# Two-layer hybrid transformer on one core: adaLN steps issued between blocks of the second product, and GpSimd's subtractions moved to VectorE

## The chip, the cores and the metric

The kernel runs on one core of a Trainium2 chip. The metric is device time in microseconds (us), the median of the runs. A profiled execution is one run with the hardware profiler on. Engines are named as in the profile: PE (TensorE), DVE (VectorE), ACT (ScalarE), POOL (GpSimd) and SP (SyncE, whose queue issues most DMAs).

## The reference, cut to what matters

```
def swiglu(h, wi, wo):
    g, u = jnp.split(h @ wi, 2, axis=-1)
    return (jax.nn.silu(g) * u) @ wo
def ffn_step(t, sh, sc, g, wi, wo):
    return t + 0.5 * g * swiglu(modulate(rms(t), sh, sc), wi, wo)
...
mod_l = (jax.nn.silu(c) @ ada_w[i] + ada_b[i])[:, None, :]     # 9 vectors of 1024: shift, scale, gate x 3
mod_c = jax.nn.silu(c_ctx) @ ada_w[i] + ada_b[i]
x = ffn_step(x, sh1, sc1, g1, pre_wi, pre_wo)                  # half-step
x = x + g2 * mixer(modulate(rms(x), sh2, sc2), ...)            # attention and its output projection
x = ffn_step(x, sh3, sc3, g3, post_wi, post_wo)                # half-step
```

This is done for two layers. The stream has 512 latent and 256 context tokens of width 1024 (the last half-step: the latent tokens alone), and the inner width of a half-step is 2816. All is float32.

## The kernel before, in words

The stream `x` stays in SBUF as 8 chunks of 128 features by 768 tokens. Each float32 factor of a product is split in a high and a low part (`split`: ACT casts the high part, DVE subtracts to get the low one, line 74 for weights), and each product is three matmuls. So every weight slab of 128x1024 costs two casts on ACT and two subtractions on DVE (tiles `whi` and `wlo`).

There are four half-steps (`ffn`): layer 0 pre and post, layer 1 pre and post. Each runs over 22 chunks `f` of the inner width. Chunk `f` of the first product is `up(f)` (tile `ps_up`). Chunks 0 to 2 use the normed activations plainly (line 522); from chunk 3 on a product with 7 in place of 8 multiplications is used (line 456), for which each chunk needs 4 sums of weight quarters (tile `s`, lines 442 to 445) and the whole half-step needs 3 sums of activation quarters (`Seven.sums`: tiles `both`, `t`, `T1` to `T3` with high and low parts, made after chunk 1, and `Seven.replace` after chunk 2). After chunks 4, 8, 12, 16 and 20 the second product `down(g)` of four earlier chunks follows (tile `ps_dn`, line 569), in four weight slabs of four blocks each; DVE adds each block to `x` times the gate (line 390). After chunk 21 comes the last `down`.

`Norm` makes a half-step's normed activations chunk by chunk while the product before it ends: DVE multiplies (`xs`), ACT adds the shift and casts (`h_h`), and the low part `h_l` is made by POOL for feature chunks 1, 3 and 5 (line 373, behind two ACT instructions) and by DVE for the others (line 376).

The adaLN vectors need a matrix-vector product with `ada_w` for two conditions. Most of it is cut into steps (`Halves`): a step loads a 128x512 piece (`wh`, by SP, three buffers) and DVE multiplies it with the conditions and sums along the row (line 253, tiles `junkh` and `wh`; two multiplies a step, one where only latent tokens need the vector). Steps are issued by `beside`, after a chunk of the first product, from chunk 1 on:

```
                halves(Q0, seven.pool)      # Q0, Q1, Q2 = 6, 4, 5 steps after each chunk 1 to 19
```

The framework orders each engine's instructions by a planned timeline; instructions marked with `keep` (the DMAs of the steps among them) keep their place in the order in which the code issues them. On each engine, and in SP's queue, instructions run in the order that results.

Of the kernel before, what the change touches and what calls it, by code (L numbers as in the profile page):

```python
# [17 lines left out]
P = 128  # L18
# [24 lines left out]
def hybrid_backbone_kernel(ctx: ExitStack, tc: tile.TileContext, I, out):  # L43
# [175 lines left out]
    class Halves:  # L219
# [6 lines left out]
        def add(self, l, ms):  # L226
            def bias(m):
                md = const.tile([P, 2, KC], F32, name=f"mod{l}_{m}")
                mods[l][m] = md[:, 0], md[:, 1], md
                b = adab[:, l, m * KC:(m + 1) * KC].unsqueeze(1).broadcast_to([P, 2, KC])  # L230
                if m in (1, 4, 7):
                    nc.gpsimd.tensor_scalar_add(md, b, 1.0)
                else:
                    nc.gpsimd.tensor_copy(md, b)

            def silu(q):
                cs = []
                for nm in ("c", "c_ctx"):
                    t = small.tile([P, 512], F32, name="ch", tag="ar", bufs=3)
# [5 lines left out]
            def job(pool, q, m, d):  # L245
# [3 lines left out]
                w = pool.tile([P, 512], F32, name="wh", tag="wh", bufs=3)  # L249
                keep(nc.sync.dma_start(w, I["ada_w"][l, m * KC + d, :, q * 512:(q + 1) * 512]))  # L250
                for ty in types:
                    o = w if ty == types[-1] else small.tile([P, 512], BF16, name="junkh", tag="tmp", bufs=4)
                    nc.vector.scalar_tensor_tensor(o, w, 1.0, self.c[ty], ALU.mult, ALU.mult,  # L253
                                                   accum_out=self.part[:, ty, d:d + 1])
                if d == KC - 1:
                    md, n = mods[l][m][2], len(types)
                    nc.gpsimd.tensor_add(md[:, :n], md[:, :n], self.part[:, :n])  # L257
                    if q == 1 and m in (2, 8):
                        nc.gpsimd.tensor_scalar_mul(md[:, :n], md[:, :n], 0.5)

            for q in range(2):
                for m in ms:
                    for d in range(KC):
                        def f(pool, q=q, m=m, d=d):
                            if q == 0 and d == 0:
                                bias(m)
                            if m == ms[0] and d == 0:
                                silu(q)
                            job(pool, q, m, d)
                        self.steps.append(f)  # L270

        def __call__(self, n, pool):
            for _ in range(min(n, len(self.steps))):
                self.steps.pop(0)(pool)

# [33 lines left out]
    class Norm:  # L309
# [53 lines left out]
        def chunk(self, p, d):  # L363
            s0, n, ty, _ = self.parts[p]
            tk = slice(s0, s0 + n)
            sh, sc = (mods[self.l][self.msh + i][ty][:, d:d + 1] for i in range(2))
            hi, lo = self.reg.hi[:, d, tk], self.reg.lo[:, d, tk]
            xs = small.tile([P, 256], F32, name="xs", tag="tmp", bufs=4)
            nc.vector.scalar_tensor_tensor(xs, x[:, d, tk], sc, self.r[p], ALU.mult, ALU.mult)  # L369
            if d % 2 and d < 7:  # L370
                nc.scalar.activation(xs, xs, AF.Identity, bias=sh)
                nc.scalar.copy(hi, xs)
                nc.gpsimd.tensor_sub(lo, xs, hi.bitcast(F32))
            else:
                nc.scalar.activation(hi, xs, AF.Identity, bias=sh)
                nc.vector.scalar_tensor_tensor(lo, xs, sh, hi.bitcast(F32), ALU.add, ALU.subtract)


    turns = [0]

    def into_x(group, pieces, gate, product, follow=None):

        slabs = [load_slab(src) for src, _ in group]
        for s0, n, ty, parts in pieces:
            for i, (_, ds) in enumerate(group):
                for dd, d in enumerate(ds):
# [5 lines left out]
                    if follow is not None:  # L392
                        for p in parts:
                            follow(p, d)


    class Seven:
# [13 lines left out]
        def sums(self, pool):  # L411
# [87 lines left out]

    def ffn(l, msh, w1, w2, nt, norm, pool, after_up, follow, side, beside=None, feed=None):  # L500

# [57 lines left out]
        def down(g):  # L559
# [4 lines left out]
            def product(ps, w, i, d, s0, n):  # L564
                for fi, f in enumerate(fs):
                    wh, wl = w.cols(fi * dper * P + i * P, P)
                    ah, al = acts[f]
                    for k, (wv, a) in enumerate(((wh, ah), (wh, al), (wl, ah))):
                        nc.tensor.matmul(ps, wv, a[:, s0:s0 + n], start=fi == 0 and k == 0,  # L569
                                         stop=fi == nf - 1 and k == 2)  # L570

            jobs = [(w2[4 * g + s], list(range(s * dper, (s + 1) * dper))) for s in range(nf)]
            last = fs[-1] == NF - 1
            for group in ([jobs] if last else [[j] for j in jobs]):
                into_x(group, parts_of(nt) if last else halves, mods[l][msh + 2], product, follow if last else None)

# [145 lines left out]

    def oproj(l, oh, ol, w, nt, norm):
        def product(ps, wt, i, d, s0, n):
# [6 lines left out]
        for ds in ([0], [1], [2], [3], [4], [5], [6, 7]):  # L731
            into_x([(w[d], [d]) for d in ds], parts_of(nt) if len(ds) > 1 else halves_of(nt), mods[l][5], product,
                   norm.follow)

# [351 lines left out]
    halves = Halves()  # L1086
    Q0, Q1, Q2 = 6, 4, 5
    h0 = Norm(0, 0, T, "right", "h0_")
# [9 lines left out]
    with tc.tile_pool(name="f0", bufs=1) as pool:  # L1098
# [47 lines left out]
        halves.add(0, (2,))  # L1146
        halves.add(0, range(3, NMOD))

        def beside(f, seven):
            if f == 0:  # L1150
                start_cm.__exit__(None, None, None)
            elif f < NF - 2:
                if f == 17:
                    load_gains(0, "a")
                    load_rest(small)
                halves(Q0, seven.pool)
        ffn(0, 0, I["pre_wi"][0], I["pre_wo"][0], T, h0, pool, up_done, h1.follow, "right", beside, feed)
# [124 lines left out]
```

## Time and profile before

| | |
|---|---|
| median of 3 runs | 2940.08 us (2938.19 to 2943.32) |
| profiled execution | 2939.59 us, span 2937.8 us |
| PE busy | 2733.8 us, 93% of the span |
| DVE busy | 2229.2 us, 76% |
| ACT, POOL busy | 1229.8 us (42%), 498.3 us (17%) |
| mean granted PE clock | 0.979 |

PE is busy nearly always, and the shares are averages over stages: what limits a stage is read from the windows and waits of that stage. The granted clock is a share of the full one: 1.0 stands for 2.4 GHz and 0.5 for 1.2 GHz.

### The profile page before, as it was taken

Reading aid. Unit: us, or ns where it says so; the run is one execution under the profiler, and the core shown is the slowest. Engines: PE = TensorE matmul, PEld = TensorE weight load, DVE = VectorE, ACT = ScalarE, POOL = GpSimd, SP = SyncE. Lnnn points to the kernel's source line nnn. Section 1 sums busy time; section 2 is a strip of 40 time slices with the busy share of each in tenths; the row PEclk is TensorE's granted clock in tenths of the full one; section 3 lists DMA queues with packets and bytes.
Section 4 is the critical chain, followed back from the end, with each engine's and each line's share of the span. In section 5 each row is a group of like instructions: output and inputs, shape, how many; then the busy total and the mean of one; then the engine's idle time right before and its main releaser. Section 6 shows DMA issues by size and latency. Waiting matters only on the chain.

```text
span 2937.8 us, 47517 instructions
## 1 busy us (share of the span) xinstructions
PE 2733.8 (93%) x17948; PEld 2589.0 (88%) x17948; DVE 2229.2 (76%) x4613; ACT 1229.8 (42%) x3053; POOL 498.3 (17%) x586
## 2 busy tenths in 40 slices
PE   4799899999999989799999989999999999999999
PEld 3698898889999978789999978999998999999999
DVE  7988987877677756877886598787766766488887
ACT  4423222336556644323333343332334566454443
POOL 5300000025433422200000051000002521220000
PEclk9899999999999999899999999999999999999999
DMA  6333433322011022233332223343322101223333
GB/s 209 114 127 129 133 125 101 119 79 73 30 30 34 26 85 73 86 108 115 109 114 65 72 76 115 126 133 112 100 73 89 45 29 30 73 78 101 98 93 101
DMA packets 98709, 266.49 MB, mean 91 GB/s; under 512 B 12592, under 2 KB 16688, under 8 KB 98352
## 3 DMA queue, kind: packets, MB, share of 16 engines
q1 hardware_dynamic: 91968, 251.78, 26.8%
q10 hardware_dynamic: 6512, 11.68, 1.2%
q8 instruction: 141, 2.31, 0.3%
q14 instruction: 88, 0.72, 0.1%
HBM read 256.07 MB, written 7.34 MB: 90 GB/s over the span
## 4 chain that ended last, share of the span: by engine, by line
PE 66%; DVE 22%; issue 4%; DMA 4%; ACT 2%; POOL 1%; SPq 0%; ACTq 0%; DVEq 0%; POOLq 0%
PE ps_up L456 24%; PE ps_dn L569 22%; PE ps_qkv L651 7%; DVE wlo L74 4%; PE ps_dn L728 4%; DVE wh L253 3%; DVE junkh L253 2%; PE ps_av L989 2%; PE ps_up L522 2%; DMA wh<-in_ada_w 2%; DVE xs L369 1%; DMA raw<-in_pre_wi 1%; PE ps_av L825 1%; PE ps_s L781 1%; PE ps_pt L978 1%
## 5 line engine op out<-in xcount | busy, mean ns | idle before, releaser
L73 ACT CAST whi<-raw 128x512 fp32r<-128x512 f32 x556 | 341.4, 620 | 765.5 <-PE ps_dn L569 318.0
L569 PE MATMUL ps_dn<-ah,whi 128*128 128x256 f32 (+1 forms) x1456 | 463.3, 321 | 2.6 <-DVE x L390 1.8
L74 DVE TENSOR_TENSOR wlo<-raw,whi 128x512 fp32r<-128x512 f32 x556 | 402.9, 729 | 79.9 <-ACT whi L73 68.4
L569 PE MATMUL ps_dn<-al,whi 128*128 128x256 f32 (+1 forms) x1456 | 462.0, 319 | 0.1
L569 PE MATMUL ps_dn<-ah,wlo 128*128 128x256 f32 (+1 forms) x1456 | 454.1, 319 | 0.2 <-DVE wlo L74 0.2
L456 PE MATMUL ps_up<-h_h,whi 128*128 128x384 f32 (+1 forms) x1216 | 400.9, 330 | 38.7 <-ACT whi L73 25.9
L456 PE MATMUL ps_up<-h_h,wlo 128*128 128x384 f32 (+1 forms) x1216 | 394.3, 328 | 12.9 <-DVE wlo L74 12.8
L456 PE MATMUL ps_up<-h_l,whi 128*128 128x384 f32 (+1 forms) x1216 | 397.8, 327 | 0.0
L390 DVE SCALAR_TENSOR_TENSOR x<-ps_dn,mod,x 128x256 f32<-128x256 f32 (+1 forms) x442 | 241.9, 556 | 142.5 <-PE ps_dn L569 101.9
L73 ACT CAST whi<-s 128x512 fp32r<-128x512 f32 x304 | 188.1, 620 | 266.9 <-PE ps_up L456 221.9
L569 PEld LDWEIGHTS ps_dn<-ah,whi 128*128 128x128 f32 x1456 | 276.1, 191 | 25.3 <-ACT whi L73 2.5
L569 PEld LDWEIGHTS ps_dn<-al,whi 128*128 128x128 f32 x1456 | 277.5, 191 | 19.6 <-DVE al L74 0.3
L569 PEld LDWEIGHTS ps_dn<-ah,wlo 128*128 128x128 f32 x1456 | 275.9, 191 | 19.4 <-DVE wlo L74 0.4
L456 PEld LDWEIGHTS ps_up<-h_h,whi 128*128 128x128 f32 x1216 | 233.1, 192 | 47.1 <-ACT whi L73 27.2
L456 PEld LDWEIGHTS ps_up<-h_h,wlo 128*128 128x128 f32 x1216 | 232.2, 192 | 15.1 <-DVE wlo L74 15.0
L74 DVE TENSOR_TENSOR wlo<-s,whi 128x512 fp32r<-128x512 f32 x304 | 208.2, 687 | 41.7 <-ACT whi L73 38.0
L456 PEld LDWEIGHTS ps_up<-h_l,whi 128*128 128x128 f32 x1216 | 233.0, 192 | 0.5
L651 PE MATMUL ps_qkv<-whi,h_h 128*128 128x256 f32 x704 | 205.4, 292 | 4.3 <-DVE a L607 3.6
L651 PE MATMUL ps_qkv<-wlo,h_h 128*128 128x256 f32 x704 | 199.7, 286 | 1.9 <-DVE wlo L74 1.9
L651 PE MATMUL ps_qkv<-whi,h_l 128*128 128x256 f32 x704 | 200.3, 285 | 0.0
L257 POOL TENSOR_TENSOR mod<-mod,part 128x16 f32<-128x16 f32 (+1 forms) x32 | 14.7, 460 | 1065.4 <-DVE wh L253 1031.5
L253 DVE SCALAR_TENSOR_TENSOR wh<-wh,ch 128x512 f32<-128x512 f32 x256 | 185.5, 733 | 1.7 <-DMA wh<-in_ada_w 1.5
(226 smaller groups left out, 6684.9 us busy)
## 6 DMA issues: line engine op xcount, KB each, us to landing
wh<-in_ada_w SPq DMA_DIRECT2D x256, 256.0 KB, 3.7
raw<-in_pre_wi SPq DMA_DIRECT2D x88, 512.0 KB, 3.5
raw<-in_post_wi SPq DMA_DIRECT2D x88, 512.0 KB, 3.5
raw<-in_pre_wo SPq DMA_DIRECT2D x44, 512.0 KB, 3.5
raw<-in_post_wo SPq DMA_DIRECT2D x44, 512.0 KB, 3.5
raw<-in_a_w_qk SPq DMA_DIRECT2D x16, 512.0 KB, 3.5
araw<-in_ada_w SPq DMA_DIRECT2D x12, 512.0 KB, 4.5
raw<-in_a_w_v SPq DMA_DIRECT2D x8, 512.0 KB, 3.5
```

The costliest lines, as they stand in the source:

```text
L73: nc.scalar.copy(hi, src)
L74: nc.vector.tensor_sub(lo, src, hi.bitcast(F32))
L253: nc.vector.scalar_tensor_tensor(o, w, 1.0, self.c[ty], ALU.mult, ALU.mult, accum_out=self.part[:, ty, d:d + 1])
L369: nc.vector.scalar_tensor_tensor(xs, x[:, d, tk], sc, self.r[p], ALU.mult, ALU.mult)
L390: nc.vector.scalar_tensor_tensor(x[:, d, s0:s0 + n], ps, gate[ty][:, d:d + 1], x[:, d, s0:s0 + n], ALU.mult, ALU.add)
L456: nc.tensor.matmul(ps, ww, z[:, k, :n], start=first and k == 0 and i == 0, stop=k == 3 and i == 2, skip_group_check=True)
L522: nc.tensor.matmul(ps, w, h[:, k, s0:s0 + n], start=k == 0 and i == 0, stop=k == KC - 1 and i == 2)
L569: nc.tensor.matmul(ps, wv, a[:, s0:s0 + n], start=fi == 0 and k == 0, stop=fi == nf - 1 and k == 2)
L651: nc.tensor.matmul(ps, h[:, k, bt], w, start=n == 0, stop=n == 23)
L728: nc.tensor.matmul(ps, wv, o[:, k, s0:s0 + n], start=k == 0 and j == 0, stop=k == KC - 1 and j == 2)
L781: nc.tensor.matmul(sv[:, u], Q[:, c, qt], K[:, c, kb0 * P + u * half:kb0 * P + (u + 1) * half], start=i == 0, stop=i == 1)
L989: nc.tensor.matmul(po[:, j], a[:, k, j], V[:, kb, g], start=k == 0, stop=k == len(kbs) - 1)
```

## The change

Steps are no longer issued in equal numbers after each chunk. `beside(first, early)` issues none after chunks 1 to `first` (3), save in the first half-step (5, 5 and 6 steps after chunks 1, 2 and 3), and one after each later chunk; `between(n)` spreads `n` steps (13, 10 and 13 in the three half-steps) over the 16 blocks of each of the first five second products. The ninth vector's 16 steps of layer 0 move from the first half-step into the output projection of the first attention, two after each of its first 8 blocks, in buffers of tag `st`. The operations of a step are as before. Apart from that, all low parts of `Norm`, the other half of the `both` sums and the low parts of `T1` to `T3` go from POOL to DVE, and `Norm`'s chunks 1, 3 and 5 lose one ACT instruction each.

```diff
-        def __call__(self, n, pool):
+        def __call__(self, n, room):
             for _ in range(min(n, len(self.steps))):
-                self.steps.pop(0)(pool)
+                self.steps.pop(0)(room)
+
+        def beside(self, first, early=()):
+            def f(i, seven):
+                if i:
+                    self(early[i - 1] if i <= len(early) else int(i > first), (seven.pool, "wh", 3))
+            return f
+
+        def between(self, n):
+            def f(i, seven):
+                self((i + 1) * n // 16 - i * n // 16, (seven.pool, "wh", 3))
+            return f
...
-            if d % 2 and d < 7:
-                nc.scalar.activation(xs, xs, AF.Identity, bias=sh)
-                nc.scalar.copy(hi, xs)
-                nc.gpsimd.tensor_sub(lo, xs, hi.bitcast(F32))
-            else:
-                nc.scalar.activation(hi, xs, AF.Identity, bias=sh)
-                nc.vector.scalar_tensor_tensor(lo, xs, sh, hi.bitcast(F32), ALU.add, ALU.subtract)
+            nc.scalar.activation(hi, xs, AF.Identity, bias=sh)
+            nc.vector.scalar_tensor_tensor(lo, xs, sh, hi.bitcast(F32), ALU.add, ALU.subtract)
...
                     if follow is not None:
                         for p in parts:
                             follow(p, d)
+                    if tick is not None:
+                        tick()
...
-                    (nc.vector if i else nc.gpsimd).tensor_add(r[:, :2 * n], self.hi[:, kk, :2 * n].bitcast(F32),
+                    nc.vector.tensor_add(r[:, :2 * n], self.hi[:, kk, :2 * n].bitcast(F32),
                                          self.lo[:, kk, :2 * n].bitcast(F32))
...
                     nc.scalar.copy(th[:, k, :n], t)
-                    nc.gpsimd.tensor_sub(tl[:, k, :n], t, th[:, k, :n].bitcast(F32))
+                    nc.vector.tensor_sub(tl[:, k, :n], t, th[:, k, :n].bitcast(F32))
...
+            blocks = iter(range(16))
+            def tick():
+                if between is not None and fs[-1] < NF - 1:
+                    between(next(blocks), seven)
...
-        halves.add(0, range(3, NMOD))
+        halves.add(0, range(3, NMOD - 1))
+        others = halves.beside(3, (5, 5, 6))
...
-        oproj(0, o.hi, o.lo, I["a_w_o"], T, h2)
+        halves.add(0, (NMOD - 1,))
+        oproj(0, o.hi, o.lo, I["a_w_o"], T, h2, lambda: halves(2, (pool, "st", 5)))
...
-            lambda f, seven: halves(Q1, seven.pool) if 0 < f < NF - 2 else None)
+            halves.beside(3), halves.between(10))
...
-            lambda f, seven: halves(Q2, seven.pool) if 0 < f < NF - 2 else None)
+            halves.beside(3), halves.between(13))
```

What this does to the order is seen at three places. On DVE in the second half-step, at chunks 1 to 3, the quarter sums (`t`, `both`) stood among adaLN multiplies before:

```order
L427 TENSOR_TENSOR t<-both,t 128x384
L424 TENSOR_TENSOR t<-both 128x384
L253 SCALAR_TENSOR_TENSOR wh,part<-wh,ch 128x512 x2
L253 SCALAR_TENSOR_TENSOR junkh,part<-wh,ch 128x512
L425 TENSOR_TENSOR t<-both,t 128x384
L555 TENSOR_TENSOR sg<-sg,ps_up 128x512
L426 TENSOR_TENSOR t<-both 128x384
L74 TENSOR_TENSOR wlo<-raw,whi 128x512
L253 SCALAR_TENSOR_TENSOR wh,part<-wh,ch 128x512
```

Now the same sums stand there without multiplies, and with the low parts `T1l` to `T3l` that POOL made before:

```order
L438 TENSOR_TENSOR t<-both,t 128x384
L439 TENSOR_TENSOR t<-both 128x384
L437 TENSOR_TENSOR t<-both 128x384
L443 TENSOR_TENSOR T1l<-t,T1h 128x384
L74 TENSOR_TENSOR al<-sg,ah 128x256
L440 TENSOR_TENSOR t_12694<-both,t 128x384
L443 TENSOR_TENSOR T2l<-t,T2h 128x384
L74 TENSOR_TENSOR wlo<-raw,whi 128x512
L438 TENSOR_TENSOR t<-both,t 128x384
L443 TENSOR_TENSOR T3l<-t,T3h 128x384
```

Second, on DVE in the same half-step at the end of chunk 12, just ahead of a second product (its first `x` is the first block's sum), there was no multiply before:

```order
L483 TENSOR_TENSOR u<-u,ps_up 128x384
L74 TENSOR_TENSOR wlo<-raw,whi 128x512
L485 TENSOR_TENSOR u<-u,ps_up 128x384
L74 TENSOR_TENSOR wlo<-raw,whi 128x512
L487 TENSOR_TENSOR u<-u,ps_up 128x384
L74 TENSOR_TENSOR wlo<-raw,whi 128x512
L465 TENSOR_TENSOR u<-u 128x384
L74 TENSOR_TENSOR al<-u,ah 128x384
L491 TENSOR_TENSOR u<-u,ps_up 128x384
L74 TENSOR_TENSOR wlo<-raw,whi 128x512
L390 SCALAR_TENSOR_TENSOR x<-ps_dn,mod_8_2888,x 128x512
```

Now most multiplies of the steps that the code issues inside that second product stand ahead of it, where 16 of them lie between chunk 11's and chunk 12's last addition of a product (the line that was 487 and is now 504):

```order
L255 SCALAR_TENSOR_TENSOR wh,part<-wh,ch 128x512 x2
L255 SCALAR_TENSOR_TENSOR junkh,part<-wh,ch 128x512
L255 SCALAR_TENSOR_TENSOR wh,part<-wh,ch 128x512
L255 SCALAR_TENSOR_TENSOR junkh,part<-wh,ch 128x512
L500 TENSOR_TENSOR u<-u,ps_up 128x384
L255 SCALAR_TENSOR_TENSOR junkh,part<-wh,ch 128x512
L74 TENSOR_TENSOR wlo<-raw,whi 128x512
L255 SCALAR_TENSOR_TENSOR wh,part<-wh,ch 128x512
L478 TENSOR_TENSOR u<-u 128x384
L255 SCALAR_TENSOR_TENSOR wh,part<-wh,ch 128x512
L504 TENSOR_TENSOR u<-u,ps_up 128x384
L74 TENSOR_TENSOR wlo<-raw,whi 128x512
```

Third, in SP's queue around a second product of the first half-step, the four weight slabs (`raw` from `pre_wo`) were mostly loaded one behind the other before:

```order
L94 DMA raw<-in_pre_wo 128x1024
L250 DMA wh<-in_ada_w 128x512 x3
L94 DMA raw<-in_pre_wo 128x1024 x3
L94 DMA raw<-in_pre_wi 128x1024 x2
L250 DMA wh<-in_ada_w 128x512 x5
```

Now three pieces of `ada_w` stand between each two of them:

```order
L94 DMA raw<-in_pre_wo 128x1024
L252 DMA wh<-in_ada_w 128x512 x3
L94 DMA raw<-in_pre_wo 128x1024
L252 DMA wh<-in_ada_w 128x512 x3
L94 DMA raw<-in_pre_wo 128x1024
L252 DMA wh<-in_ada_w 128x512 x3
L94 DMA raw<-in_pre_wo 128x1024
```

## Rows read from the trace of the kernel before

**Rows 1.** The page: busy time of each engine; DVE's busy tenths in 40 slices.

```profile
PE 2733.8 (93%) x17948; PEld 2589.0 (88%) x17948; DVE 2229.2 (76%) x4613; ACT 1229.8 (42%) x3053; POOL 498.3 (17%) x586
...
DVE  7988987877677756877886598787766766488887
```

**Rows 2.** Stretches: length; busy PE, PEld, DVE, ACT, POOL; PE clock; DMA share; GB/s.

```profile
171.70:575.80 404.10, 379.72 (x2114) 356.62 (x2112) 334.59 (x756) 126.22 (x228) 5.36 (x10) 0.98 0.38 120
1253.70:1630.40 376.70, 367.37 (x2076) 346.05 (x2075) 292.67 (x601) 123.00 (x222) 3.15 (x7) 1.00 0.32 101
1816.10:2187.80 371.70, 366.11 (x2080) 346.45 (x2080) 276.85 (x546) 122.84 (x222) 3.65 (x9) 1.00 0.34 111
2095.20:2187.80 92.60, 92.48 (x530) 88.26 (x529) 59.83 (x104) 31.06 (x56) 0.00 (x0) 1.00 0.23 69
1061.90:1136.00 74.10, 72.06 (x460) 65.25 (x458) 26.92 (x46) 20.44 (x45) 17.97 (x22) 0.98 0.21 61
84.40:145.10 60.70, 43.49 (x238) 37.63 (x237) 57.99 (x111) 20.49 (x43) 23.27 (x16) 0.87 0.36 109
1137.70:1218.30 80.60, 63.04 (x356) 55.43 (x356) 76.79 (x139) 35.39 (x78) 33.71 (x27) 0.87 0.26 79
1717.00:1784.60 67.60, 53.67 (x295) 46.50 (x294) 65.73 (x116) 26.81 (x59) 29.94 (x23) 0.90 0.29 94
2560.00:2613.50 53.50, 44.22 (x300) 42.32 (x300) 46.98 (x81) 28.28 (x65) 24.38 (x24) 0.84 0.21 68
575.80:615.30 39.50, 38.21 (x218) 33.93 (x218) 28.89 (x64) 8.47 (x16) 0.48 (x2) 1.00 0.27 81
```

**Rows 3.** PE's waits from 58 to 2262 us: total us, times, longest.

```profile
PE ps_up L456 <- ACT whi L73: 30.2, 11, 12.5
PE ps_up L456 <- DVE wlo L74: 18.4, 7, 4.9
PE ps_up L456 <- ACT u L464: 12.9, 14, 2.2
PE ps_up L456 <- DVE u L483: 10.8, 12, 3.3
```

**Rows 4.** Chain that ended last, first half-step: start us, us, what.

```profile
257.14 14.76 PE ps_up L456 x82
```

**Rows 5.** Timeline, second half-step, chunks 1 to 3: start us, us, instruction, [idle before].

```profile
1200.10 1.19 POOL L430 TENSOR_TENSOR T2l<-t,T2h 128x384 fp32r<-128x384 f32 x1 [1.03 <-ACT T2h L429]
...
1200.34 1.50 DVE L253 SCALAR_TENSOR_TENSOR wh<-wh,ch 128x512 f32<-128x512 f32 x1
...
1206.97 0.69 PE L456 MATMUL ps_up<-h_h,wlo 128*128 128x384 f32 x1 [4.77 <-DVE wlo L74]
...
1207.45 0.68 DVE L253 SCALAR_TENSOR_TENSOR junkh<-wh,ch 128x512 bf16<-128x512 f32 x1
...
1208.06 0.55 DVE L425 TENSOR_TENSOR t<-both,t 128x384 f32<-128x384 f32 x1
...
1208.53 0.55 DVE L426 TENSOR_TENSOR t<-both 128x384 f32<-128x384 f32 x1
...
1218.36 0.69 PE L456 MATMUL ps_up<-h_h,whi 128*128 128x384 f32 x1 [7.82 <-ACT whi L73]
```

**Rows 6.** Timeline of PE, third half-step, chunk 3.

```profile
1783.33 0.69 PE L456 MATMUL ps_up<-h_h,whi 128*128 128x384 f32 x1 [5.62 <-ACT whi L73]
```

**Rows 7.** Timeline of DVE, second half-step, three instructions merged in each.

```profile
1138.06 1.27 DVE L369 SCALAR_TENSOR_TENSOR xs<-x,mod,ar 128x256 f32<-128x256 f32 x3
...
1167.96 2.68 DVE L420 TENSOR_TENSOR both<-h_h,h_l 128x768 f32<-128x768 f32 x3
```

**Rows 8.** Groups of POOL by shape: xcount, busy us, mean ns, idle before.

```profile
L373 POOL TENSOR_TENSOR h_l<-xs,h_h 128x256 fp32r<-128x256 f32 x42 | 35.0, 833 | 33.4 <-ACT h_h L372 31.5 <-PE ps_up L522 1.3
...
L420 POOL TENSOR_TENSOR both<-h_h,h_l 128x768 f32<-128x768 f32 x12 | 26.4, 2209 | 5.6 <-DVE t L426 3.8 <-DVE mod L217 1.8
...
L430 POOL TENSOR_TENSOR T1l<-t,T1h 128x384 fp32r<-128x384 f32 x12 | 16.6, 1387 | 54.7 <-ACT T1h L429 54.7
```

**Rows 9.** The page's DMA issues: KB each, median us to landing.

```profile
wh<-in_ada_w SPq DMA_DIRECT2D x256, 256.0 KB, 3.7
```

More of the change, by code (lines that the diff above doesn't have):

```diff
@@ L234, in bias, with silu @@
                     nc.gpsimd.tensor_copy(md, b)
-            def silu(q):
+            def silu(room, q):
                 cs = []
                 for nm in ("c", "c_ctx"):
-                    t = small.tile([P, 512], F32, name="ch", tag="ar", bufs=3)
+                    pool, tag, bufs = (small, "ar", 3) if room[1] == "wh" else room
+                    t = pool.tile([P, 512], F32, name="ch", tag=tag, bufs=bufs)
                     keep(nc.sync.dma_start(t, I[nm][q * 512:(q + 1) * 512].partition_broadcast(P)))
@@ L243, in silu, with job @@
                 self.c = cs
-            def job(pool, q, m, d):
+            def job(room, q, m, d):
                 types = (0, 1) if l == 0 or m < 5 else (0,)
@@ L248, in job @@
                     self.part = small.tile([P, 2, KC], F32, name="part", tag="part", bufs=2)
-                w = pool.tile([P, 512], F32, name="wh", tag="wh", bufs=3)
+                pool, tag, bufs = room
+                w = pool.tile([P, 512], F32, name="wh", tag=tag, bufs=bufs)
                 keep(nc.sync.dma_start(w, I["ada_w"][l, m * KC + d, :, q * 512:(q + 1) * 512]))
@@ L263, in add, with f @@
                     for d in range(KC):
-                        def f(pool, q=q, m=m, d=d):
+                        def f(room, q=q, m=m, d=d):
                             if q == 0 and d == 0:
@@ L267, in f @@
                             if m == ms[0] and d == 0:
-                                silu(q)
-                            job(pool, q, m, d)
+                                silu(room, q)
+                            job(room, q, m, d)
                         self.steps.append(f)
-        def __call__(self, n, pool):
+        def __call__(self, n, room):
             for _ in range(min(n, len(self.steps))):
-                self.steps.pop(0)(pool)
+                self.steps.pop(0)(room)
[8 more added lines that the diff above has]
+            return f
     def rstd_steps(sq, s_n, n, use, room=None):
@@ L369, in chunk, with into_x @@
             nc.vector.scalar_tensor_tensor(xs, x[:, d, tk], sc, self.r[p], ALU.mult, ALU.mult)
-            if d % 2 and d < 7:
-                nc.scalar.activation(xs, xs, AF.Identity, bias=sh)
-                nc.scalar.copy(hi, xs)
-                nc.gpsimd.tensor_sub(lo, xs, hi.bitcast(F32))
-            else:
-                nc.scalar.activation(hi, xs, AF.Identity, bias=sh)
-                nc.vector.scalar_tensor_tensor(lo, xs, sh, hi.bitcast(F32), ALU.add, ALU.subtract)
+            nc.scalar.activation(hi, xs, AF.Identity, bias=sh)
+            nc.vector.scalar_tensor_tensor(lo, xs, sh, hi.bitcast(F32), ALU.add, ALU.subtract)
     turns = [0]
-    def into_x(group, pieces, gate, product, follow=None):
+    def into_x(group, pieces, gate, product, follow=None, tick=None):
         slabs = [load_slab(src) for src, _ in group]
@@ L498, in hybrid_backbone_kernel, with ffn @@
     EARLY = 1
-    def ffn(l, msh, w1, w2, nt, norm, pool, after_up, follow, side, beside=None, feed=None):
+    def ffn(l, msh, w1, w2, nt, norm, pool, after_up, follow, side, beside=None, between=None, feed=None):
         seven = None
@@ L574, in down @@
             for group in ([jobs] if last else [[j] for j in jobs]):
-                into_x(group, parts_of(nt) if last else halves, mods[l][msh + 2], product, follow if last else None)
+                into_x(group, parts_of(nt) if last else halves, mods[l][msh + 2], product, follow if last else None,
+                       tick)
         for f in range(NF):
@@ L720, in finish, with oproj @@
                 self.tick()
-    def oproj(l, oh, ol, w, nt, norm):
+    def oproj(l, oh, ol, w, nt, norm, tick=None):
         def product(ps, wt, i, d, s0, n):
@@ L732, in oproj @@
             into_x([(w[d], [d]) for d in ds], parts_of(nt) if len(ds) > 1 else halves_of(nt), mods[l][5], product,
-                   norm.follow)
+                   norm.follow, tick)
     def diff_attention(norm, O, pool, save, finish_proj, ready):
@@ L1086, in hybrid_backbone_kernel @@
     halves = Halves()
-    Q0, Q1, Q2 = 6, 4, 5
     h0 = Norm(0, 0, T, "right", "h0_")
@@ L1151, in beside @@
                 start_cm.__exit__(None, None, None)
-            elif f < NF - 2:
+            else:
                 if f == 17:
@@ L1155, in beside @@
                     load_rest(small)
-                halves(Q0, seven.pool)
-        ffn(0, 0, I["pre_wi"][0], I["pre_wo"][0], T, h0, pool, up_done, h1.follow, "right", beside, feed)
+                if f < NF - 1:
+                    others(f, seven)
+        ffn(0, 0, I["pre_wi"][0], I["pre_wo"][0], T, h0, pool, up_done, h1.follow, "right", beside, halves.between(13), feed)
     o = attention_phase(0, h1, T)
```

## The prediction

> **What bounds the kernel now.** I read the page first: PE is busy 93% of the span, VectorE 76%, but VectorE's slices run from 6 to 9 tenths [rows 1], so the question is which stages wait for it. PE's waits say it: in the stretch with the first three half-steps, the longest sums end with weights that ACT or VectorE prepares (30.2 and 18.4 us) and with ACT's and VectorE's work on the products (12.9 and 10.8) [rows 3]. ACT is no bound (42%); its casts wait for VectorE's quarter sums. The windows then show two kinds of stage [rows 2].
>
> Steady cycles: four chunks of the first product and one second product. The cycle from 2095.2, which has no adaLN step, takes 92.6 us with PE busy 92.48. Four of them would take 370.4. The first half-step's four, with 6 steps beside nearly every chunk, take 404.1: 33.7 us too many, with VectorE busy 335 of them. In the second and third half-step (4 and 5 steps a chunk) PE idles 376.7 - 367.4 = 9.3 and 371.7 - 366.1 = 5.6.
>
> Starts, where the quarter sums of the activations are made beside chunks 1 to 3: VectorE is busy 58.0 of 60.7, 76.8 of 80.6 and 65.7 of 67.6 us there, and PE waits 4.77 and then 7.82 us for the first two weights of chunk 3 in the second half-step [rows 5], 5.62 in the third [rows 6]. The granted clock is 0.87 to 0.90 in these windows, against 1.00 in undisturbed cycles, so part of the matmuls after such a wait run at half rate.
>
> **What the change costs and saves on VectorE.** Issued back to back, a multiply of a step takes 0.61 us (1207.45 to 1208.06), a subtraction of 384 columns 0.47 [rows 5], one of 768 0.89, a norm operation of 256 0.42 [rows 7]. But the multiply that starts 0.24 us after GpSimd's T2l took 1.50 us, where 0.68 is usual, and ended 0.55 after it: it was held up until GpSimd was done [rows 5]. In the second half-step's start I count in the order 24 multiplies, 39 norm operations, 20 of 384, 4 of 768, 19 of 512 and 9 smaller; at 0.60 for 512 and 0.32 for the small ones they need 14.6 + 16.4 + 9.4 + 3.6 + 11.4 + 2.9 = 58.3 us, and VectorE was busy 76.8. The other 18.5 is delay beside GpSimd, whose 25 instructions there go to VectorE for 9 x 0.42 + 4 x 0.89 + 12 x 0.47 = 13.0 us, in place of 0.83, 2.21 and 1.39 us each on GpSimd [rows 8].
>
> The Trainium skill, SBUF — State Buffer, section "SBUF: two separate sides", says that VectorE with two SBUF inputs and GpSimd take their shared port pair as an exclusive lock for a whole instruction. The row agrees in kind. By the rule the loss could reach 9 x 0.83 + 4 x 2.21 + 12 x 1.39 = 33 us in this start, against the 18.5 that the windows give; the sum would gain no more by it, since PE becomes the bound there before.
>
> Term 1, steady cycles: 33.7 + 9.3 + 5.6 = 48.6 us can be won. In the first half-step the last 14 of the 16 moved steps leave these cycles, and in all three the rest stands mostly in the chunk ahead of a second product and beside the blocks. I leave 1 us for each of the 12 cycles: 48.6 - 12 = 36.6. If VectorE stays late as often as now, nothing is won: bounds 0 and 48.6.
>
> Is there room for the hoisted group? Between the last additions of chunks 11 and 12 VectorE now has 16 multiplies, 9.8 us, beside 8 us of its usual work, so some 18 us, where a chunk takes PE 14.8 [rows 4]. It falls 3 us behind there, but the two weights that the second product begins with stand before the bulk of the group, and its first slab feeds four blocks, a quarter of a second product of 92.6 - 4 x 14.76 = 33.6 us: 8.4 us of cover. If that cover is gone, 3 us come back each time.
>
> Term 2, start of the second half-step: out go 24 multiplies (14.6) and the 18.5 of delay, in come 13.0. VectorE's 76.8 becomes 56.7, with the 3.8 it idled 60.5, so it reaches the second weights of chunk 3 at 1137.7 + 60.5 = 1198, where PE arrives at about the same time as now (it began chunk 3 at 1201.7). PE runs the first of seven products (2.1 us), then meets five subtractions still ahead of it (3 us): second product at 1204, not 1218.4, 14.4 earlier. The group of multiplies ahead of the first second product comes right behind this without cover built up; I give back 1.0. Gain 13.4, bounds 7 and 20 (all idle time from 1136 to 1253).
>
> Term 3, third half-step: 23 multiplies (14.0) leave and the delay, 65.7 less the 48.6 that the order's instructions need, counted in the same way, 17.1; 10.8 comes. VectorE arrives 20 us earlier, at 1764, before PE can (1775.6 less what PE waits in chunks 0 to 2, some 9). Second product at 1767 + 5 = 1772, against 1783.3, less 1.3: gain 10, bounds 5 and 17.
>
> Term 4, first half-step: it keeps 16 of its 18 steps beside chunks 1 to 3, so 31 multiplies stand there for 32; 9.2 of low parts come, 58.0 - 44.9 (counted likewise) = 13.1 of delay goes: 4.5 earlier. Behind it, 18 multiplies stand beside chunk 4. Bounds -3 and 10.
>
> Term 5, last half-step: no steps, but the same sums and norm. PE idles 9.3 of 53.5 us at clock 0.84 [rows 2]. I take a third, 3, bounds 0 and 7. Term 6, the norms that lead into the two attentions lose one ACT instruction and a GpSimd subtraction of 0.83 us [rows 8] per odd chunk: 2, bounds 0 and 4.
>
> At nothing: the 16 steps in the output projection are 32 x 0.61 = 19.5 us of VectorE, which idles 47 of that window's 74.1 [rows 2]; uncovered they would cost 19.5. DMA bytes are unchanged.
>
> Sum: 36.6 + 13.4 + 10 + 4.5 + 3 + 2 = 69.5. The profiled execution's own time is 2939.59 (1.8 over its span, 0.5 under the median of the runs shown), so 2939.6 - 69.5 = **2870**. All upper bounds give 48.6 + 20 + 17 + 10 + 7 + 4 = 107, so 2833; all lower ones 0 + 7 + 5 - 3 + 0 + 0 = 9, so 2931.
>
> **The rivals.** (a) The groups of multiplies ahead of the 15 second products are not covered: VectorE is 3 to 6 us late at each, say 3, so 45 come back: 2915. For it: the multiplies are issued between blocks, but the order puts most of them before, so the change does less than it says; and single chunks lose time now at 18 to 19 us of VectorE work. Against it: the slack of 8.4 us. (b) VectorE's stretched instructions have another cause than GpSimd, and it is simply full. Then the delays of 18.5, 17.1 and 13.1 stay: 69.5 - 48.7 = 21, so 2919. The Trainium skill, Perfetto Trace Analysis, section "Optimizing Scalar/DVE Operations", speaks for this side: when VectorE is saturated, work may be offloaded to GpSimd; it adds that their shared port can undo that, which the 1.50 us row shows. (c) Slower: in SP's queue a weight slab of the second product now stands behind three adaLN pieces, and each of these waits until VectorE has emptied its buffer; a piece lands 3.7 us after its issue [rows 9]. With 15 second products of three later slabs each, a slab late by 69.5 / 45 = 1.5 us eats all; at 3 us late the time is 2939 + 66 = 3005. Against it: the second product from 575.8 already runs with three pieces between slabs, and PE idles 1.3 us of 39.5 in it [rows 2]. (d) More: the cycles become clean and the starts lose their slow clock: 2845 or less.
>
> **How the numbers follow.** Forecast, gain 50 to 90: 0.60. (d) 0.13. (a), partly or whole, 0.14; (b) 0.06; (c) 0.05; no change that could be measured 0.02. A measurement of this kernel tells about 0.2%, 6 us, from no change. So faster 0.93, same 0.02, slower 0.05. The range leaves out the ends of (d), (c) and part of (a) and (b): 2838 to 2910.
>
> **What would show it.** Right: adaLN multiplies absent from chunks 1 to 3 of the second and third half-step, no quarter sum on GpSimd, VectorE's multiplies back at 0.68 us there, PE's wait for chunk 3's second weights under 2 us, cycles of 93 to 95 us, clock near 1.0 after chunk 0. Wrong: waits of the second product's first matmuls for `wlo` or of VectorE for pieces of `ada_w`, or PE idle around chunks 4, 8, 12 and 16. What makes it wrong is most likely the first term: if the hoisted group costs 3 us a cycle more or less than I think, the sum moves by 36.

## The result, and the profile after

The median fell from 2941.7 to 2862.76 us (4 runs each, 2859.42 to 2867.81 after): a ratio of 0.9734, 95% interval 0.9714 to 0.9754. The prediction was 2870, with 2838 to 2910 as its range. The profiled execution took 2867.81 us with a span of 2866.0, 71.8 less than before.

The page of the changed kernel (busy time and share of the span; PE clock in 40 slices) answers to [rows 1]: PE went from 93 to 95%, VectorE's busy time fell by 22 us although it took over GpSimd's work, and GpSimd lost 124 us.

```profile
PE 2711.5 (95%) x17948; PEld 2575.4 (90%) x17948; DVE 2207.1 (77%) x4719; ACT 1218.0 (42%) x3015; POOL 373.8 (13%) x480
...
PEclk9899999999999999999999999999999999999999
```

Where the time came from is read by stages. Second products begin at a slightly different point of chunk 4 now, so I cut at their ends. In the windows of the kernel before (columns as in [rows 2]), the rows are: first half-step up to the end of its first second product, then to the end of its fifth ("cycles"); the output projection; start and cycles of the second half-step, of the third, and the start of the fourth.

```profile
58.60:209.75 151.15, 125.27 (x648) 111.61 (x648) 136.15 (x264) 56.47 (x104) 35.12 (x23) 0.93 0.39 122
209.75:615.25 405.50, 379.83 (x2112) 356.41 (x2112) 335.70 (x757) 126.73 (x230) 5.83 (x12) 0.98 0.37 119
...
1061.90:1139.10 77.20, 74.20 (x468) 66.47 (x466) 29.76 (x53) 22.15 (x49) 19.13 (x23) 0.98 0.22 66
1139.10:1284.65 145.55, 126.22 (x699) 114.63 (x700) 122.97 (x234) 53.12 (x110) 33.94 (x28) 0.91 0.28 86
1284.65:1668.05 383.40, 374.06 (x2114) 352.37 (x2113) 291.48 (x593) 124.96 (x226) 3.15 (x7) 1.00 0.31 98
...
1704.90:1847.70 142.80, 126.36 (x712) 113.82 (x712) 121.18 (x223) 52.48 (x110) 38.29 (x33) 0.94 0.31 102
1847.70:2225.40 377.70, 372.11 (x2114) 352.15 (x2113) 276.94 (x543) 124.85 (x226) 3.06 (x8) 1.00 0.33 107
...
2564.80:2657.40 92.60, 86.57 (x659) 84.89 (x660) 79.10 (x146) 44.70 (x98) 22.28 (x22) 0.92 0.23 75
```

The same stages of the changed kernel:

```profile
58.90:209.45 150.55, 125.39 (x646) 110.25 (x647) 131.81 (x284) 56.20 (x104) 10.26 (x7) 0.91 0.37 123
209.45:593.00 383.55, 375.07 (x2114) 354.54 (x2113) 315.72 (x689) 127.46 (x229) 4.36 (x9) 0.99 0.36 114
...
1037.50:1121.00 83.50, 76.94 (x470) 68.61 (x469) 52.48 (x119) 25.76 (x56) 23.58 (x26) 0.96 0.43 128
1121.00:1240.90 119.90, 116.78 (x699) 107.99 (x700) 105.68 (x227) 49.12 (x100) 1.02 (x2) 0.99 0.28 87
1240.90:1624.50 383.60, 374.12 (x2114) 354.51 (x2113) 299.30 (x625) 124.38 (x226) 4.12 (x8) 0.99 0.32 103
...
1661.30:1785.90 124.60, 119.44 (x713) 108.19 (x712) 109.18 (x227) 51.21 (x103) 6.22 (x7) 1.00 0.30 96
1785.90:2157.75 371.85, 370.82 (x2115) 352.62 (x2114) 280.46 (x563) 125.11 (x226) 4.30 (x10) 1.00 0.35 116
...
2497.90:2585.60 87.70, 84.76 (x661) 82.78 (x662) 76.02 (x169) 41.53 (x92) 0.87 (x1) 0.96 0.25 79
```

The starts of the second and third half-step give 25.7 and 18.2 us, and their clock goes from 0.91 and 0.94 to 0.99 and 1.00. The first half-step's cycles give 22.0, the third's 5.9. Three rows disappoint: the first half-step's start (0.6), the second's cycles (none), and the projection, which takes 6.3 us more.

PE's waits in the first three half-steps, against [rows 3], say why (us in total, times, longest). Of the old long waits for prepared weights one is left, 15.4 us, at chunk 3 of the first half-step, where the kernel before waited 4.74 and then 12.47 us. New at the second place is PE's wait for VectorE's addition to `x`, that is, for a bank that the second product can write.

```profile
PE ps_up L469 <- ACT whi L73: 15.4, 1, 15.4
PE ps_dn L583 <- DVE x L401: 14.6, 10, 4.1
```

The longest of these is in the second half-step. VectorE's timeline ahead of its third second product (start, us, instruction, idle before it):

```profile
1396.79 0.69 DVE L255 SCALAR_TENSOR_TENSOR wh<-wh,ch 128x512 f32<-128x512 f32 x1
1397.40 0.08 DVE L255 DVE_READ_ACCUMULATOR wh<-wh,ch 128x1 f32 x1
1397.40 0.69 DVE L255 SCALAR_TENSOR_TENSOR wh<-wh,ch 128x512 f32<-128x512 f32 x1
1398.02 0.08 DVE L255 DVE_READ_ACCUMULATOR wh<-wh,ch 128x1 f32 x1
1400.55 0.69 DVE L255 SCALAR_TENSOR_TENSOR junkh<-wh,ch 128x512 bf16<-128x512 f32 x1 [2.45 <-DMA wh<-in_ada_w]
...
1406.34 0.74 DVE L401 SCALAR_TENSOR_TENSOR x<-ps_dn,mod,x 128x512 f32<-128x512 f32 x1
```

and PE's, a moment later:

```profile
1407.23 0.76 PE L583 MATMUL ps_dn<-ah,whi 128*128 128x512 f32 x1 [4.09 <-DVE x L401]
1407.79 0.63 PE L583 MATMUL ps_dn<-al,whi 128*128 128x512 f32 x1
```

Sixteen multiplies stand in front of that first addition. VectorE runs its instructions in their order: it waits 2.45 us for a piece, and the addition, whose block was ready at 1400.91, comes at 1406.34. Four blocks fit PE's banks, and the fourth was done at 1403.14, so PE stands still for 4.09 us. The cycle around it takes 100.0 us, its neighbours 94.2 and 95.3.

My theory for the experiments was therefore: what the change still loses, and part of what the kernel before loses, comes from multiplies that the planner puts ahead of work that PE is about to need. The rivals: VectorE is simply full; the waits for pieces are what costs; or the place of the steps in the code matters, not their order.

### The profile page after: what moved, and what is told of

Same layout as the page of the kernel before. It is cut to its first block, busy times and chain, and to the rows that moved or that the text cites. A ratio compares the mean times of both kernels' runs of the same rounds, so it can differ in the third digit from the quotient of the medians.

```text
span 2866.0 us, 47324 instructions
## 1 busy us (share of the span) xinstructions
PE 2711.5 (95%) x17948; PEld 2575.4 (90%) x17948; DVE 2207.1 (77%) x4719; ACT 1218.0 (42%) x3015; POOL 373.8 (13%) x480
## 4 chain that ended last, share of the span: by engine, by line
PE 73%; DVE 15%; DMA 5%; issue 3%; ACT 2%; POOL 2%; SPq 0%; ACTq 0%; DVEq 0%; POOLq 0%
PE ps_up L469 28%; PE ps_dn L583 22%; PE ps_qkv L672 7%; PE ps_up L536 6%; DMA wh<-in_ada_w 3%; DVE wlo L74 3%; PE ps_dn L749 2%; PE ps_av L1010 2%; DVE wh L255 2%; DVE junkh L255 1%; PE ps_av L846 1%; PE ps_s L802 1%; DMA raw<-in_pre_wi 1%; PE ps_pt L999 1%; DVE xs L384 1%
## 5 line engine op out<-in xcount | busy, mean ns | idle before, releaser
L583 PE MATMUL ps_dn<-ah,whi 128*128 128x256 f32 (+1 forms) x1456 | 467.3, 324 | 15.7 <-DVE x L401 14.6
L74 DVE TENSOR_TENSOR wlo<-raw,whi 128x512 fp32r<-128x512 f32 x556 | 388.5, 704 | 81.2 <-ACT whi L73 63.9
L255 DVE SCALAR_TENSOR_TENSOR wh<-wh,ch 128x512 f32<-128x512 f32 x256 | 173.8, 690 | 17.3 <-DMA wh<-in_ada_w 17.1
```

The costliest lines, as they stand in the source:

```text
L74: nc.vector.tensor_sub(lo, src, hi.bitcast(F32))
```

## The experiments

Each was timed in five rounds beside the kernel before. Ratios are to that kernel.

**One part alone.** The first takes the kernel before and moves only the low parts and sums:

```diff
-                    (nc.vector if i else nc.gpsimd).tensor_add(r[:, :2 * n], ...
+                    nc.vector.tensor_add(r[:, :2 * n], ...
-                    nc.gpsimd.tensor_sub(tl[:, k, :n], t, th[:, k, :n].bitcast(F32))
+                    nc.vector.tensor_sub(tl[:, k, :n], t, th[:, k, :n].bitcast(F32))
```

and the norms as in the change. 

> The kernel before, with only the subtractions and sums of GpSimd (quarter sums and norms) moved to VectorE; the steps stay where they were. By the prediction's terms (VectorE is held up beside GpSimd) the starts of the first three half-steps lose 13.1, 18.5 and 17.1 us of delay for 9.2, 13.0 and 10.8 us of new work, the last half-step gains some 3 and the norms 2: 20 us less, 2921. By rival (b) (VectorE is simply full) the delay stays and the new work comes on top: 33 us more, 2974.

Measured: 2920.23, ratio 0.9938 (0.9923 to 0.9953): 19.7 us, as the sum of the terms had it. Rival (b) falls. The parts agree less well: by the profiles the three starts, up to the end of each first second product, give 9.8 of it, where the terms had 15.7, and the first of them gives nothing; 3.8 come in the first half-step's cycles and 3.2 in the attention and projection.

The second is the changed kernel with these lines as before. 

> The changed kernel, with the quarter sums and norm parts back on GpSimd as before; only the steps have their new places. If the two parts add up (72 us in all, 20 from the moves) this gives 52 us: 2890. If the moves only pay where no multiplies stand, or the multiplies were most of what was held up, the two overlap: 60 us or more, 2880 or less. By rival (b) the moves cost 33 and this is the better kernel: 2830.

Measured: 2884.78, ratio 0.9817 (0.9799 to 0.9835): 55 us from the steps. The two parts add up (19.7 + 55.2 = 74.9; the changed kernel gained 78.9 beside its own kernel before, and each ratio is good to some 5 us).

The third puts only the norms back. 

> The changed kernel, with the low parts of the norms for feature chunks 1, 3 and 5 back on GpSimd, behind two ACT instructions; the quarter sums stay on VectorE. The moves together were worth 22 us on top of the steps (2884.8 against 2862.8). If each part counts by its GpSimd time in a start (9 x 0.83 of 33 us), the norms are worth 5, and 2 in the attentions: 2868 to 2870. Rival: the norms stand on the path of chunk 0, where PE waits for low parts, and the quarter sums behind cover: half or more of the 22, 2874 to 2880.

Measured: 2865.16, ratio 0.9737 (0.9723 to 0.9751), which cannot be told from the changed kernel and is below both ranges that I expected. The moves pay through the quarter sums; the low parts of the norms are worth nothing that shows.

**The order of the multiplies.** One edit on the changed kernel:

```diff
-                    nc.vector.scalar_tensor_tensor(o, w, 1.0, self.c[ty], ALU.mult, ALU.mult,
-                                                   accum_out=self.part[:, ty, d:d + 1])
+                    keep(nc.vector.scalar_tensor_tensor(o, w, 1.0, self.c[ty], ALU.mult, ALU.mult,
+                                                        accum_out=self.part[:, ty, d:d + 1]))
```

> The changed kernel, with the steps' multiplies held in the order in which the code issues them, so that they run between the blocks and not ahead of the second product. Theory: multiplies put ahead wait for pieces of ada_w (2.45 us at 1398.1) and the additions behind them leave PE without a bank (4.09 us at 1403.1); that costs 12 us of idle PE in the first three half-steps and some slow clock behind it: 10 to 17 us less than the changed kernel, 2850. Rival: the waits for pieces move into the second products and hold up its additions there, or VectorE is late with the next chunk's weights: 2863 to 2885.

Measured: 2823.46, ratio 0.9606 (0.9589 to 0.9623): 39 us below the changed kernel, where I expected 10 to 17, and the best version. Its windows, first half-step's start and cycles, then the second's:

```profile
59.10:191.50 132.40, 122.27 (x650) 108.28 (x651) 122.79 (x257) 55.78 (x105) 9.44 (x7) 0.95 0.40 129
191.50:569.80 378.30, 370.99 (x2111) 351.77 (x2111) 323.48 (x712) 126.97 (x230) 3.35 (x9) 1.00 0.37 119
...
1095.30:1213.60 118.30, 117.11 (x702) 108.35 (x703) 103.04 (x217) 48.93 (x100) 1.02 (x2) 0.99 0.27 87
1213.60:1583.80 370.20, 369.56 (x2114) 353.13 (x2112) 303.18 (x635) 126.14 (x227) 2.91 (x8) 1.00 0.33 107
```

The second half-step's cycles lose 13.4 us and the first's 5.3, where the theory put the gain. The rest is mostly the first half-step's start, 18.2. There VectorE made the last weight sum of chunk 3 and PE waited, in the changed kernel and then in this one:

```profile
137.25 0.68 DVE L458 TENSOR_TENSOR s<-raw,s 128x512 f32<-128x512 f32 x1
...
138.69 0.69 PE L469 MATMUL ps_up<-h_h,whi 128*128 128x384 f32 x1 [15.41 <-ACT whi L73]
```

```profile
123.80 0.68 DVE L458 TENSOR_TENSOR s<-raw,s 128x512 f32<-128x512 f32 x1
...
125.24 0.44 PE L469 MATMUL ps_up<-h_h,whi 128*128 128x384 f32 x1 [2.49 <-ACT whi L73]
```

The cast waits for VectorE's weight sums `s`. In VectorE's order 29 multiplies stood ahead of the last of these sums in the changed kernel, and 7 stand there now: most of the steps that the code issues behind chunks 1 to 3 had been put ahead of it.

The next keeps the planner's order and takes the steps from between the blocks; 5, 4 and 5 go after each chunk from 4 on:

```diff
-                    self(early[i - 1] if i <= len(early) else int(i > first), (seven.pool, "wh", 3))
+                    self(early[i - 1] if i <= len(early) else n * int(i > first), (seven.pool, "wh", 3))
...
-            halves.beside(3), halves.between(10))
+            halves.beside(3, n=4))
```

> The changed kernel, without steps between blocks: from chunk 4 on 5, 4 and 5 steps are issued after each chunk of the three half-steps, none after chunks 1 to 3 (first half-step as changed). If the steps between blocks are worth something, the cycles go back towards those of before (idle PE 9.2 and 5.5 us in the second and third, some 16 in the first, against 9.4, 1.0 and 8.5): 2863 + 12 and some slow clock, 2875 to 2885. If only the emptied chunks 1 to 3 count, 2857 to 2869.

Measured: 2886.18, ratio 0.9822 (0.9804 to 0.9839). So in the planner's order the steps between blocks are worth 23 us (26 by the ratios). With the multiplies of that kernel in code order:

> The kernel of the fourth experiment (no steps between blocks, 4 or 5 after each chunk from 4 on: 2886), with the multiplies in code order. If the order is what costs (multiplies put ahead of the work that PE waits for), the place in the code matters little: 2823 to 2835. If steps between blocks are needed, since a chunk of 14.8 us has no room for 6.1 us of multiplies, half or more of the 23 us between 2886 and 2863 stays on top of 2823: 2835 to 2850.

Measured: 2829.37, ratio 0.9619 (0.9605 to 0.9633): within 6 us of the best. In code order the place hardly matters; a chunk has room for 5 steps. And the kernel before, with nothing but this edit:

> The kernel before, with nothing but its multiplies held in code order. If multiplies put ahead were what cost in its cycles as well, most of the 48.6 us of term 1 is won: 2895 to 2910. If its delays come from GpSimd's sums and from the number of steps beside chunks 1 to 3, the order alone gives little: 2925 to 2945.

Measured: 2863.78, ratio 0.9735 (0.9721 to 0.9749). I had expected 45 us of it at most; it gives 79, as much as the whole change. The rows are its first half-step's start and cycles, the second's, and the third's.

```profile
59.60:202.00 142.40, 127.38 (x650) 112.79 (x651) 129.68 (x240) 55.92 (x105) 34.43 (x23) 0.93 0.38 123
202.00:583.30 381.30, 371.68 (x2111) 353.15 (x2110) 341.82 (x781) 127.83 (x230) 6.46 (x12) 1.00 0.40 128
...
1103.60:1235.60 132.00, 124.72 (x699) 113.80 (x700) 117.03 (x218) 53.12 (x110) 31.86 (x28) 0.94 0.29 93
1235.60:1606.00 370.40, 369.94 (x2114) 353.05 (x2113) 294.49 (x609) 124.63 (x227) 2.80 (x7) 1.00 0.32 102
1642.20:1778.20 136.00, 122.77 (x713) 109.07 (x713) 117.67 (x214) 52.58 (x113) 39.62 (x32) 0.99 0.31 103
1778.20:2150.60 372.40, 370.67 (x2113) 352.69 (x2113) 278.01 (x553) 124.34 (x227) 3.93 (x9) 1.00 0.34 110
```

Its cycles are as good as those of the best version, with 6, 4 and 5 steps beside nearly every chunk: what they lost was lost to order, not to the amount of work. What it lacks is in the starts (142.4, 132.0, 136.0 against 132.4, 118.3, 123.9): there the emptied chunks or GpSimd's subtractions count, and a run below tells which.

**A group put ahead in the code.** The version in code order, with 8 of each second product's steps issued one chunk earlier, so that 16 to 18 multiplies stand in front of it again:

```diff
-                    self(early[i - 1] if i <= len(early) else int(i > first), (seven.pool, "wh", 3))
+                    self((early[i - 1] if i <= len(early) else int(i > first)) + 8 * (i % 4 == 3), (seven.pool, "wh", 3))
```

and `n - 8` in place of `n` between the blocks. 

> The kernel with the multiplies in code order (2823.5), but with 8 of the steps of each second product issued one chunk earlier, after chunks 3, 7, 11, 15 and 19: 16 to 18 multiplies stand in front of each second product again, as in the changed kernel, only by the code. Theory: such a group holds up the additions of the second product; what the changed kernel loses in its cycles against the kernel in code order (12.8 us in three cycles of the second half-step, some 5 in the first, 2 in the third) comes back: 2838 to 2850. Rival: what cost in the changed kernel was something else that the order of the multiplies brought with it (the weights of chunk 3 in the first half-step, the projection): 2820 to 2832.

Measured: 2841.93, ratio 0.9669 (0.9653 to 0.9685): 18 us come back, as expected, but only in part where I expected them. By the profiles, 7.8 of them are in the second half-step's cycles and 3.6 in the third's; the first half-step's cycles, for which I had some 5, give nothing (377.9 against 378.3). 5 stand in the attention, where the steps are the same, and I can't say why; so the range was met partly by luck. The wait for a bank is back, at the same second product as in the changed kernel, and ahead of it VectorE waited for a piece:

```profile
1376.94 0.69 DVE L255 SCALAR_TENSOR_TENSOR junkh<-wh,ch 128x512 bf16<-128x512 f32 x1 [2.98 <-DMA wh<-in_ada_w]
...
1382.90 0.76 PE L583 MATMUL ps_dn<-ah,whi 128*128 128x512 f32 x1 [3.00 <-DVE x L401]
```

The same without the pieces' loads (one for each set of steps is left; since its piece is used again, all products are written to `junkh`):

```diff
+                if d == 0 and m == ms[0]:
+                    self.w = pool.tile([P, 512], F32, name="wh", tag=tag, bufs=bufs)
+                    keep(nc.sync.dma_start(self.w, I["ada_w"][l, m * KC + d, :, q * 512:(q + 1) * 512]))
+                w = self.w
```

> The same as the kernel with the group ahead in code order, but without the loads of the steps (work left out: one piece of ada_w is loaded for each set of steps and multiplied again and again). If VectorE's waits for pieces are what makes the group expensive, the cost goes: 2820 to 2828. If it is the mass of 16 multiplies (9.8 us) in front of the additions, it stays: within 5 us of the kernel with the group ahead.

Measured: 2855.15, ratio 0.9716 (0.9703 to 0.9729). Without the loads it is not faster; it is 13 us slower, and that I had not expected. By the profile some 11 of it lie in the first half-step's start, where PE waits 7.72 us at chunk 3 and, after VectorE's 3.32 us for the first piece of a new set, 4.97 for a bank; the order of its loads differs, so this start is no clean comparison. The cycles are: 382.4 in the second half-step against 378.0 with the loads. The wait in the third second product is there too, 3.75 us, and so is VectorE's wait ahead of it, for the one piece that this set of steps still loads:

```profile
1384.51 0.69 DVE L257 SCALAR_TENSOR_TENSOR junkh<-wh,ch 128x512 bf16<-128x512 f32 x1 [3.34 <-DMA wh<-in_ada_w]
...
1393.05 0.77 PE L585 MATMUL ps_dn<-ah,whi 128*128 128x512 f32 x1 [3.75 <-DVE x L403]
```

So the run took the loads away everywhere but at the place that costs most, and it does not clear the waits for pieces. What it shows is that the mass of multiplies alone costs little: the other three cycles, without a long wait for a piece, take 93.9 to 94.0 us against 92.2 to 93.5 in code order. In all three kernels the dear place is where the steps go over from the first half of the condition vectors (`ch`) to the second. The second load of the new vectors waits 4.2 us in SP's queue of the changed kernel for the old ones' last multiply, and later pieces queue behind it. The cycle there takes 100.0, 97.2 and 100.5 us with the group ahead, and 92.2 in code order. That is read from the traces; no run takes this one load away.

**Three smaller ones**, all on the version in code order. The quarter sums and norms back on GpSimd: 

> The kernel with the multiplies in code order, with quarter sums and norm parts back on GpSimd. The moves were worth 20 us alone and 22 on top of the steps. If they are worth that whatever the order of the multiplies (VectorE's other work at the starts is held up too): 2843 to 2847. If it was the multiplies that were held up beside GpSimd, and in code order none stand at the starts of the second and third half-step: 2825 to 2833.

Measured: 2856.67, ratio 0.9723 (0.971 to 0.9736). The moves are worth 33 us here, more than either expectation. Since no multiplies stand in chunks 1 to 3 of the second and third half-step, VectorE's other work is held up as well. 14 of the 33 are in the first half-step's start, where the early steps stand beside the sums; PE waits 2.27 and 4.43 us there for a bank in the first second product. This kernel and the kernel before in code order (ratio 0.9735) differ in the places of the steps alone, and their intervals overlap: 7 us by the medians, 4 by the ratios. So in code order the new places are worth next to nothing by themselves, and the moves make most of the 40 us from there to the best version. The old places with the moves, in code order, were not run.

The ninth vector's steps out of the output projection and into the first half-step's second products (`between(16)`): 

> The kernel with the multiplies in code order (2823.5), and the ninth vector's 16 steps taken out of the output projection of the first attention, into the second products of the first half-step (16 steps in each, one behind each block, in place of 13). Theory: the projection took 83.5 us with the steps and 77.2 without, so 5 to 7 us come back, and VectorE has room for three more steps in each second product: 2817 to 2819. Rival: VectorE, busy 79 of 93 us in a cycle there, has no room for 3.7 us more, and the additions come late: 2823 to 2835.

Measured: 2826.28, ratio 0.9609 (0.9595 to 0.9622), the same as with them: the gain did not come, and the time is in the rival's range. The profiles show 2 us less from the first half-step's fifth second product to the second half-step, and 3 us more in the first half-step's cycles.

The early steps spread over four chunks, `(3, 4, 4, 5)`: 

> The kernel with the multiplies in code order, with the 16 early steps of the first half-step spread over four chunks, 3, 4, 4 and 5 after chunks 1 to 4, in place of 5, 5 and 6 after 1 to 3. PE waits 3.5 us for chunk 3's weights there, with 3.4 us at the low clock behind: 3 to 5 us less, 2819 to 2821, and the best version. Rival: the gate that these steps make is needed by the first second product, behind chunk 4; it comes later than the product's first block, and 0 to 6 us are lost: 2824 to 2830.

Measured: 2834.62, ratio 0.9644 (0.963 to 0.9657): 11 us worse, by the rival's mechanism and twice its price. The first addition of the first second product needs the gate that these steps make:

```profile
177.64 0.77 PE L583 MATMUL ps_dn<-ah,whi 128*128 128x512 f32 x1 [11.64 <-DVE x L401]
```

## Why the prediction was right

The total came within 8 us because errors of both signs met, and that is luck in part. By its terms, forecast and measured (spans of the windows above; the norms by the attentions' spans, 446.65 to 444.50 and 339.40 to 340.15 us):

| term | forecast | measured |
|---|---|---|
| 1, cycles of the three half-steps | 36.6 | 22.0 - 0.2 + 5.9 = 27.7 |
| 2, start of the second half-step | 13.4 (7 to 20) | 25.7 |
| 3, start of the third | 10 (5 to 17) | 18.2 |
| 4, start of the first | 4.5 | 0.6 |
| 5, last half-step | 3 | 4.9 |
| 6, norms into the attentions | 2 | 1.4 (the run with the norms back: none that shows) |
| projection | 0 | -6.3 |

**Rival (b) and the port.** VectorE was held up by GpSimd, not full. Its instructions that ran beside one of GpSimd's took 136 us longer in all than the median of like ones alone in the kernel before, and 70 us longer after (worked out from the two traces). The moves alone were forecast at 48.7 less 33 of new work, and 3 and 2 more, so 20.7 us, and gave 19.7. The Trainium skill, SBUF — State Buffer, section "SBUF: two separate sides", has the lock for a whole instruction, and these runs agree in kind. The Trainium skill, Perfetto Trace Analysis, section "Optimizing Scalar/DVE Operations", says that with a saturated VectorE offloading work to GpSimd may make sense, and warns that the shared port can undo it; here leaving the sums and low parts there cost 20 to 33 us, so in this case the warning decides.

**Terms 2 and 3 were mis-sized.** I let PE wait 3 us and more for subtractions ahead of chunk 3's second weights; PE does not wait there now. (What I gave back for the group ahead of the first second product, 1.0 and 1.3, came as 1.27 in the second half-step and 0.6 in the third.) And I counted only waits, not the clock. By the windows, of the 25.7 us in the second half-step's start 16.2 are idle time (span less PE's busy time, 19.3 before and 3.1 after) and 9.4 are the same matmuls in less busy time, with the granted clock at 0.99 in place of 0.91; of the 18.2 in the third, 11.3 and 6.9.

**Term 1 failed in the step "is there room for the hoisted group?"** I set 3 us of lateness against 8.4 us of cover, the time of PE's four blocks. But PE works on the four (two of 512 columns, two of 256) in turns, so that the first is done shortly before the last. In the dear second product these are the first matmul, the pair of which the first is the last of the first block (it ends at 1400.91), and the last of the fourth block:

```profile
1390.44 0.39 PE L583 MATMUL ps_dn<-ah,whi 128*128 128x512 f32 x1
...
1400.52 0.62 PE L583 MATMUL ps_dn<-ah,wlo 128*128 128x512 f32 x2
...
1402.86 0.28 PE L583 MATMUL ps_dn<-ah,wlo 128*128 128x256 f32 x1
```

So the cover is 2.2 us, from 1400.91 to 1403.14, and the addition came 5.4 us late. VectorE's wait of 2.45 us for a piece had ended just before, at 1400.55, and had put all behind it back. In code order too the first block is done 9.7 us after the product's start and the fourth 12.7, so there are 3 us of cover; there the addition begins 0.2 us after its block is done. So rival (a) is true in part: in the second half-step it ate the whole gain, in the third, where most steps have one multiply, next to nothing. The premise of the term, that the cycles lose time because steps stand beside nearly every chunk, failed as well: the kernel before in code order has them there still, and its cycles are 42.5 us shorter. I had seen that most multiplies stand ahead of the block for which the code issues them, and asked only what that costs at second products. The dearest place was another: chunk 3 of the first half-step, where multiplies put ahead kept 18 us that term 4 took as part of the start.

**The projection** was put at nothing, with VectorE idle for 47 of 74 us as cover. VectorE is busy 52.5 of 83.5 us now, and still PE waits 2.67 us for one low part, and the window's clock is 0.96 for 0.98. Idle time on average is no cover where the steps come in a lump. The pieces' loads are part of it: from its first to its last matmul the projection takes 72.7 us in two kernels in code order without steps there, 80.6 with them, and 77.1 with the multiplies but without the loads.

**Rival (c)** did not come: PE waits 0.6 us in all for a slab's cast in the second products of the changed kernel. **Rival (d)** needed what one more line gives: in code order the cycles are clean and the time is 2823.

## What to carry to other kernels

Where a planner orders an engine that runs in order, filler that is ready early is put ahead of work that another engine will soon need; before moving such filler about in the code, hold it in code order and see what is left. The same line on the old kernel was worth as much as this whole change. And here work with operands in the memory that VectorE and GpSimd share was not divided by dividing the instructions: the seemingly spare engine made the busy one slower by more than it took off.

## What was not expected of the hardware

VectorE instructions with an operand in PSUM were not held up beside GpSimd: an addition to `x` of 256 columns took 0.48 us beside GpSimd and 0.48 alone, while the subtraction `wlo`, 0.69 alone, took up to 2.83 beside it. And a stall costs well beyond itself: after the 4.09 us wait above, PE's matmuls of 512 columns follow each other at 0.43 us for some 5 us, where 0.23 is usual; the granted clock from 1407.23 to 1412.50 was 0.50, the lower of its two levels (1.2 GHz).
